# Sixteen column pairs of the last FFN's first product by Strassen, with weight sums made partly by DMA

## Chip, cores and metric

The kernel runs on one core of a Trainium2 chip. The metric is device time in microseconds, the median of the runs shown. Before the change it is 1356.94 us over three runs, 1356.64 to 1357.12.

## What is computed

A trunk of two layers on a sequence of 512 tokens with a model width of 1024: a gated short convolution, an FFN, an SSD mixer, an FFN, each between RMSNorms and with shift, scale and gate from a conditioning vector. The change lies in the last FFN alone, whose width DFF is 2816:

```python
def swiglu_ffn(h, w_in, w_out):
    gate, up = jnp.split(h @ w_in, 2, axis=-1)
    return (jax.nn.silu(gate) * up) @ w_out
```

All data are float32. The kernel splits each operand of a matmul into a high part rounded to the narrower fp32r and a low part (value minus high part), and adds three matmuls (high x high, high x low, low x high) for each product.

## The kernel before

The features of the first product lie on partitions, the 512 tokens along the free dimension. `w_in` has 22 gate and 22 up chunks of 128 columns. A chunk is `in_chunk` (L289): eight k tiles of 128 rows, each with three matmuls of 128x512 (`mm3`, L276 to L278), 24 in all. Six chunks are begun while the sub-layer before ends (the lead, `li`) and finished by `rest(i)` with 256-wide matmuls; two more (`more`) have weights ready; the last FFN's own loop (L1661 on) does the others, 38 whole chunks together with those two.

For each pair of chunks `load_pair` loads 1 MB of weights with one DMA from the SP queue into a buffer of the pool `wst` (two buffers), in rows of 256 columns. ACT copies a chunk's weights to their high part (L221), DVE subtracts for the low part (L222), into a buffer of the pool `whl` (four buffers). `gate` (L1583) puts the SiLU of a finished chunk on ACT, `up` (L1591) multiplies on DVE into `raw`, and after each fourth chunk `s13` (L1587) makes two differences of halves of `raw` on DVE. These are the first operands of the second product.

The second product, `raw` times `w_out`, is already done in the Strassen-Winograd form: seven products (`PRODUCTS`, L1537) over eleven pairs p of row blocks, 77 steps taken two at a time (`products(n)`, n from 0 to 38), each step six matmuls of 128x512 (L1650). The weights' sums t1, t2, t3 and t4 are made in place in SBUF: t1, t2 and t4 by DMAs from the POOL queue that add what they carry to what lies there (L1657), t3 by loading two blocks of `w_out` a second time, one on the ACT queue (L1664), one added from the POOL queue. `w_prep(n)` and `a_prep(n)` split the operands on ACT and DVE (L1615, L1616, L1628, L1629), four and three tiles ahead. `behind(n)` places the sums and the ends of the output blocks.

`w_out` is 11.5 MB. Before the change units 0, 1 and 2 (pairs 0 to 4; tiles `w2t0` to `w2t2`) are loaded during the loop, units 3 and 4 into `wst` buffers near its end, and units 5 to 10 into the space of the activations `h` when the last chunk has read them (L1710).

In this stage the order of the work is written out by hand: a `manual_schedule` holds for PE, SP, ACT, DVE and POOL, so each engine does its instructions in the order of the source and waits for each in turn. The pools `fo` and `fb` of this stage take the space of the phase that closes with the lead.

Of the kernel before, what the change touches and what calls it, by code (L numbers as in the profile page):

```python
# [8 lines left out]
F32 = mybir.dt.float32  # L9
# [7 lines left out]
P = 128  # L17
# [18 lines left out]
def trunk_kernel(  # L36
# [252 lines left out]
    def in_chunk(w, h):  # L289
        pst = mm_ps("ip")  # L290
        mm_chunk(pst, w, h)
        return pst
# [277 lines left out]
    with ExitStack() as ph:  # L570
# [112 lines left out]
        with tc.manual_schedule(engines={PE_ENGINE, mybir.EngineType.SP, mybir.EngineType.Activation,  # L683
# [858 lines left out]
    with ExitStack() as ph:  # L1542
# [4 lines left out]
        NP = NF // 2  # L1547
        ws, splits, gates = list(more), [(), ()], {}
# [11 lines left out]
        def w2_load(i):  # L1560

            u = units[i]
            t = w2t[i] if i < 3 else wst_p.tile([P, 1, 2, D], F32, tag="wst", name="w2s")
            for q in range(len(u)):
                dma(t[:, q, :, :], w2_rows(u[q])[:, 0])
            rows_of[i] = (t[:, :, 0, :], t[:, :, 1, :])

# [11 lines left out]

        def load_pair(p):  # L1580
            ws.extend(load_w([(w1, p % 2 * DFF + (4 + p // 2 * 2) * P, 256)], later=splits))

        def gate(f, pst):  # L1583
# [6 lines left out]

        def up(f, pst):  # L1591
            dve.tensor_mul(raw[:, f, :], pst, gates[f])
            if f % 4 == 3:
                s13(f // 2 - 1, 2)
            elif f == NF - 1:
                s13(f // 2, 1)


# [54 lines left out]
        with tc.manual_schedule(engines={PE_ENGINE, mybir.EngineType.SP, mybir.EngineType.Activation,  # L1653
                                         mybir.EngineType.DVE, mybir.EngineType.Pool}):

            def add_(dst, src):
                pool.dma_start(dst, src, accum_op=ADD)  # L1657

            def t1(i):
                add_(b_(i, "b12"), b_(i, "b11"))  # L1660

            def t3_load(i):
                for q, p in enumerate(units[i]):
                    dma_s(b_(i, "b11", q), w2_rows(p)[:, 0, 0, T:])  # L1664

            def t3(i):
                for q, p in enumerate(units[i]):
                    add_(b_(i, "b11", q), w2_rows(p)[:, 0, 1, T:])

# [5 lines left out]

            load_pair(0)
# [3 lines left out]
            tiles = []  # L1680
            K = 2 * NF - 6
            for k in range(K):
                if k % 2 == 0 and k < K - 4:
                    load_pair(k // 2 + 1)
                if k in (8, 14, 20):
                    w2_load((8, 14, 20).index(k))
                if k in (K - 4, K - 2):
                    w2_load(3 + (k - K + 4) // 2)
                if k in (K - 12, K - 10, K - 8):
                    t1((k - K + 12) // 2)  # L1690
                tiles.append(in_chunk(ws[k], h))
                q, j = divmod(k - 3, 4)
                if j < 2 and k > 2:
                    gate(4 + 2 * q + j, tiles[k - 1])
                elif k:
                    up(2 + 2 * q + j, tiles[k - 1])
                if k < K - 2:
                    for op in splits[k + 2]:
                        op()
                else:  # L1700
                    a_prep(k - K + 2)
                    w_prep(k - K + 2)
            up(NF - 1, tiles[-1])
# [4 lines left out]
            for c, r in ((0, 0), (0, 1), (1, 0), (1, 1)):  # L1708
                for i in range(5, len(units)):
                    dma(rows_of[i][r][:, 0, c * T:(c + 1) * T], w2_rows(units[i][0])[:, 0, r, c * T:(c + 1) * T])  # L1710
            for n in (2, 3):
                w_prep(n)
            a_prep(2)
            for i in range(3, len(units)):
                t1(i)
# [27 lines left out]
            def behind(n):  # L1743

                for i, u in enumerate(units):
                    if n - 8 == u[-1] // 2:
                        t2_(i)
                    if n == 8 + i:
                        t3_load(i)
                    if n == 17:  # L1750
                        t3(i)
                if n == 18:
                    for i in range(len(units)):
                        t4(i)
                for t in range(2):
# [85 lines left out]
```

## Time and profile before

| what | before |
|---|---|
| median of 3 runs | 1356.94 us |
| profiled execution: span | 1355.3 us |
| granted TensorE clock, mean | 0.997 |
| lead's last matmuls / first products' loop | until 1032.1 / 1032.1 to 1238.6 us |
| second product and end | 1238.6 to 1355.3 us |

The span runs from the first to the last instruction of one profiled execution; the median of the runs lies 1.6 us above it, which is the time around the span. PE is TensorE's matmul, PEld its weight load, DVE the vector engine, ACT the scalar engine, POOL GpSimd; SP issues most DMAs. In a group's row stand the line, the engine, the operation, the tile written and those read, the shapes, the count, then busy time and mean ns, then the engine's idle time before and what ended it. Windows give the busy time (and count) of each engine in a stretch of the span. Times in a timeline are start and duration in microseconds.

### The profile page before, as it was taken

Reading aid. Unit: us, or ns where it says so; the run is one execution under the profiler, and the core shown is the slowest. Engines: PE = TensorE matmul, PEld = TensorE weight load, DVE = VectorE, ACT = ScalarE, POOL = GpSimd, SP = SyncE. Lnnn points to the kernel's source line nnn. Section 1 sums busy time; section 2 is a strip of 40 time slices with the busy share of each in tenths; the row PEclk is TensorE's granted clock in tenths of the full one; section 3 lists DMA queues with packets and bytes.
Section 4 is the critical chain, followed back from the end, with each engine's and each line's share of the span. In section 5 each row is a group of like instructions: output and inputs, shape, how many; then the busy total and the mean of one; then the engine's idle time right before and its main releaser. Section 6 shows DMA issues by size and latency. Waiting matters only on the chain.

```text
span 1355.3 us, 17419 instructions
## 1 busy us (share of the span) xinstructions
PE 1339.1 (99%) x6909; PEld 1126.9 (83%) x6909; DVE 898.7 (66%) x1437; ACT 570.1 (42%) x893; POOL 47.0 (3%) x61
## 2 busy tenths in 40 slices
PE   8999999999999999999999999999999999999996
PEld 6788889888888888898888888888899888888885
DVE  5588866777777322658988998897673233336877
ACT  5333355232222211655554455564472212224664
POOL 0000000000000000000000000000000000001231
PEclk9999999999999999999999999999999999999998
DMA  9757760777786323415434334323311455326685
GB/s 311 233 180 231 247 202 4 242 237 245 227 257 201 110 94 94 128 33 162 137 122 128 107 96 132 117 78 121 129 62 63 156 171 172 98 96 196 159 148 120
DMA packets 160565, 204.77 MB, mean 151 GB/s; under 512 B 6868, under 2 KB 112228, under 8 KB 159460
## 3 DMA queue, kind: packets, MB, share of 16 engines
q1 hardware_dynamic: 148512, 176.34, 41.2%
q0 software_dynamic: 6240, 11.54, 5.1%
q10 hardware_dynamic: 5732, 15.79, 3.6%
q8 instruction: 54, 0.88, 0.3%
q14 instruction: 27, 0.22, 0.1%
HBM read 192.75 MB, written 2.24 MB: 144 GB/s over the span
## 4 chain that ended last, share of the span: by engine, by line
PE 93%; issue 2%; SPq 2%; DMA 1%; DVE 1%; ACT 1%; POOL 0%; DVEq 0%; POOLq 0%; ACTq 0%
PE ip L276 19%; PE ip L278 18%; PE ip L277 18%; PE y L378 6%; PE y L379 6%; PE y L380 6%; PE cA L1650 3%; PE li L276 3%; PE li L278 3%; PE li L277 3%; PE li L756 1%; PE yd L1283 1%; PE cD L1650 1%; SPq L611 1%; PE yo L1277 1%
## 5 line engine op out<-in xcount | busy, mean ns | idle before, releaser
L276 PE MATMUL ip<-h,whl 128*128 128x512 f32 x1096 | 431.1, 393 | 0.2 <-DVE cv L863 0.2
L278 PE MATMUL ip<-h,whl 128*128 128x512 f32 x1096 | 427.2, 390 | 0.0
L277 PE MATMUL ip<-h,whl 128*128 128x512 f32 x1096 | 426.8, 389 | 0.0
L222 DVE TENSOR_TENSOR whl<-wst,whl 128x1024 fp32r<-128x1024 f32 x132 | 160.7, 1221 | 133.4 <-ACT whl L221 133.2
L276 PEld LDWEIGHTS ip<-h,whl 128*128 128x128 f32 x1096 | 205.9, 188 | 43.9 <-issue 1.8
L278 PEld LDWEIGHTS ip<-h,whl 128*128 128x128 f32 x1096 | 205.8, 188 | 43.2
L277 PEld LDWEIGHTS ip<-h,whl 128*128 128x128 f32 x1096 | 206.0, 188 | 41.8
L221 ACT CAST whl<-wst 128x1024 fp32r<-128x1024 f32 x132 | 136.6, 1042 | 32.5 <-PE ip L278 23.7
L124 DVE SCALAR_TENSOR_TENSOR ada_acc<-ada_st,csil,ada_acc 128x512 f32<-128x512 f32 x140 | 105.0, 750 | 3.5
L204 DVE TENSOR_TENSOR whlo<-wsto,whlo 128x1024 fp32r<-128x1024 f32 x41 | 49.9, 1224 | 78.5 <-ACT whlo L203 78.4
L276 PE MATMUL li<-h,whl 128*128 128x256 f32 x288 | 83.3, 289 | 0.0
L278 PE MATMUL li<-h,whl 128*128 128x256 f32 x288 | 81.7, 284 | 0.0
L277 PE MATMUL li<-h,whl 128*128 128x256 f32 x288 | 81.6, 283 | 0.0
L203 ACT CAST whlo<-wsto 128x1024 fp32r<-128x1024 f32 x41 | 42.6, 1049 | 76.5 <-PE y L380 71.3
L378 PE MATMUL y<-whlo,ff 128*128 128x512 f32 x176 | 68.7, 390 | 0.0
L380 PE MATMUL y<-whlo,ff 128*128 128x512 f32 x176 | 68.5, 389 | 0.0
L379 PE MATMUL y<-whlo,ff 128*128 128x512 f32 x176 | 68.5, 389 | 0.0
L1142 DVE SCALAR_TENSOR_TENSOR cu<-ip,cols,cu 128x511 f32<-128x511 f32 (+2 forms) x84 | 62.8, 748 | 3.9 <-ACT cu L1139 1.4
L1585 ACT ACTIVATE g<-ip 128x512 f32<-128x512 f32 x18 | 10.8, 598 | 122.1 <-PE ip L278 122.1
L1650 PE MATMUL cA<-whlo,ao 128*128 128x512 f32 x264 | 61.1, 390 | 0.8 <-ACT whlo L1615 0.8
L1650 PEld LDWEIGHTS cA<-whlo,ao 128*128 128x128 f32 x264 | 49.5, 188 | 11.4 <-ACT whlo L1615 1.2
L276 PEld LDWEIGHTS li<-h,whl 128*128 128x128 f32 x288 | 55.3, 192 | 0.0
(281 smaller groups left out, 1928.2 us busy)
## 6 DMA issues: line engine op xcount, KB each, us to landing
ada_st<-in_ada_w_dram SPq DMA_DIRECT2D x96, 512.0 KB, 5.0
wst<-in_f_w_in_dram SPq DMA_DIRECT2D x44, 1024.0 KB, 5.9
wst<-in_m_w_in_dram SPq DMA_DIRECT2D x14, 1024.0 KB, 5.3
wsto<-in_f_w_out_dram SPq DMA_DIRECT2D x10, 1024.0 KB, 5.0
wst<-in_m_w_in_dram SPq DMA_DIRECT2D x20, 512.0 KB, 5.1
wst<-in_a_w_in_dram SPq DMA_DIRECT2D x9, 1024.0 KB, 6.0
csb<-cs_d ACTq DMA_DIRECT2D x8, 1024.0 KB, 5.5
wsto<-in_m_w_out_dram SPq DMA_DIRECT2D x7, 1024.0 KB, 6.5
```

The costliest lines, as they stand in the source:

```text
L124: dve.scalar_tensor_tensor(acc, w, csil[:, k:k + 1], acc, MUL, ADD)
L204: dve.tensor_tensor(dst[:, 1, :nk, :], src, dst[:, 0, :nk, :].bitcast(F32), SUB)
L221: later.append((lambda sw=sw, w=w: act.copy(w[:, 0, :nk, :], sw), lambda sw=sw, w=w: dve.tensor_tensor(w[:, 1, :nk, :], sw, w[:, 0, :nk, : ...
L222: lambda sw=sw, w=w: dve.tensor_tensor(w[:, 1, :nk, :], sw, w[:, 0, :nk, :].bitcast(F32), SUB)))
L276: pe.matmul(dst, w_at(w, 0, kk), a[:, 0, sl], start=start, stop=False)
L277: pe.matmul(dst, w_at(w, 0, kk), a[:, 1, sl], start=False, stop=False)
L278: pe.matmul(dst, w_at(w, 1, kk), a[:, 0, sl], start=False, stop=stop)
L378: pe.matmul(pst, a[:, 0, tk], wt[:, 0, kk, :], start=k == 0, stop=False)
L379: pe.matmul(pst, a[:, 0, tk], wt[:, 1, kk, :], start=False, stop=False)
L380: pe.matmul(pst, a[:, 1, tk], wt[:, 0, kk, :], start=False, stop=k == K - 1)
L1142: dve.scalar_tensor_tensor(u[:, sft:], pst[:, :T - sft], w[3 - sft], u[:, sft:], MUL, ADD)
L1650: pe.matmul(bank[r][sub], a[:, al, q, tk], w[:, hl, q, :], start=first and k == 0, stop=last and k == 2, skip_group_check=True)
```

## The change

Sixteen column pairs (units u = 0 to 15, even u gate columns, odd u up columns) of the first product are computed by seven products of 12 matmuls of 128x256 each, over halves of k, of the pair's columns and of the tokens. Four chunks and the two of `more` stay as they were.

For the moving operands the activations are added up again from their two parts (`value`), combined to four new operands T and split (`t_one` to `t_four`); two raw quadrants of `h` serve as the others. For the weights X is the first chunk, Y, S and Z are sums. `fetch(u)` issues up to five DMAs from SP in rows of 128 columns, and two adding DMAs from POOL; two more sums are made on DVE (`sum_y`, `sum_s`). Z's chunk is loaded a second time, one unit later. The accumulators are gathered by ACT and DVE (`keep`, `c11`, `c12`, `c22`, `c21`).

The T operands and the sums take the space of `w2t0` to `w2t2`, so all of `w_out` is loaded from the end of unit 15 on, by quadrants in the order of their use. t3 becomes a subtraction on POOL (b22 after t2, minus b11), and its second loads go.

```diff
-        w2t = [fb.tile([P, 2, 2, D], F32, tag=f"w2t{i}", name=f"w2t{i}") for i in range(2)]
-        w2t += [fb.tile([P, 1, 2, D], F32, tag="w2t2", name="w2t2")]
+        tq = [fb.tile([P, 2, 2, 4, 256], F32R, tag=f"w2t{i}", name=f"tq{i}") for i in range(2)]
+        sums_w = fb.tile([P, 2, 2, 4, P], F32, tag="w2t2", name="sg")
...
+        def fetch(u):
+
+            st, sg = wst_p.tile([P, 16, P], F32, tag="wst", name="wsu"), sums_w[:, u % 2]
+            staged[u] = st, sg
+            if u < UN:
+                dma(sg[:, 0], w1_cols(u, 1, 0))
+                dma(sg[:, 1], w1_cols(u, 1, 1))
+            if u:
+                dma(st[:, 8:12, :], w1_cols(u - 1, 1, 0))
+            dma(st[:, 0:8, :], w1_cols(u, 0))
+            if u:
+                dma(st[:, 12:16, :], w1_cols(u - 1, 1, 1))
+            if u < UN:
+                add_(flat2(sg[:, 0]), flat2(sg[:, 1]))
+            if u:
+                add_(flat2(st[:, 8:12, :]), flat2(staged[u - 1][0][:, 0:4, :]))
...
+        def split(dst, src):
+            act.copy(dst[:, 0], src)
+            dve.tensor_tensor(dst[:, 1], src, dst[:, 0].bitcast(F32), SUB)
...
+        def sum_y(u):
+            st, sg = staged[u]
+            dve.tensor_add(sg[:, 1], sg[:, 0], st[:, 0:4, :])
...
+            dst, w = banks[r, u][:, LO], wts[kind, u]
+            for k in range(4):
+                for i, (wl, al) in enumerate(((0, 0), (0, 1), (1, 0))):
+                    pe.matmul(dst, w[:, wl, k0 + k, :], moving(q, k, al), skip_group_check=True,
...
-            def t3(i):
-                for q, p in enumerate(units[i]):
-                    add_(b_(i, "b11", q), w2_rows(p)[:, 0, 1, T:])
+            def t3(p):
+                i = unit_of[p]
+                q = units[i].index(p)
+                pool.tensor_tensor(b_(i, "b11", q), b_(i, "b22", q), b_(i, "b11", q), SUB)
...
             for i, f in ((0, 0), (2, 0), (1, 1), (3, 1), (4, 2), (5, 3)):
                 rest(i)
-                (up if i in (2, 3) else gate)(f, lead_ps[i])
...
+                if i in (2, 3):
+                    up(f, lead_ps[i])
+                else:
+                    gate(f, lead_ps[i])
+                if i == 1:
+                    for j in range(4):
+                        value(j)
+                elif i == 3:
+                    t_one()
+                elif i == 4:
+                    for j in range(4, 8):
+                        value(j)
+            acc = in_chunk(more[0], h)
+            split_x(0)
+            for b in range(2):
+                t_two(b)
+            sum_y(0)
+            split_y(0)
+            t_three()
+            fetch(1)
+            acc2 = in_chunk(more[1], h)
+            sum_s(0)
+            up(2, acc)
+            split_s(0)
+            for u in range(UN):
...
+                    fetch(u + 2)
...
+                product(u, "P1")
+                if u:
+                    c12(v)
+                else:
+                    up(3, acc2)
+                    for b in range(2):
+                        t_four(b)
+                split_x(u + 1)
+                if u:
+                    product(v, "P7")
+                keep(u, "A", 0, LO)
+                product(u, "P5")
+                if u:
+                    c22(v)
+                product(u, "P2")
+                keep(u, "C", 1, HI)
+                if u:
+                    product(v, "P4")
+                c11(u)
+                split_z(u)
+                if not last:
+                    sum_y(u + 1)
+                    sum_s(u + 1)
+                product(u, "P6")
+                if u:
+                    c21(v)
...
+                    split_y(u + 1)
+                product(u, "P3")
+                keep(u, "A", 0, HI)
+                if not last:
+                    split_s(u + 1)
```

More of the change, by code (lines that the diff above doesn't have):

```diff
@@ new lines, in out_of, with keep, c11, c12 @@
+        def out_of(u, f):
+            if (u, f) not in outs:
+                outs[u, f] = raw[:, 4 + u // 2 * 2 + f, :] if u % 2 else t2("g")
+            return outs[u, f]
+        def keep(u, r, f, part):
+            act.copy(out_of(u, f)[:, part], banks[r, u][:, LO])
+        def c11(u):
+            dve.tensor_add(out_of(u, 0)[:, LO], banks["B", u][:, LO], out_of(u, 0)[:, LO])
+        def c12(u):
+            o, f = out_of(u, 0), 4 + u // 2 * 2
+            dve.tensor_add(o[:, HI], banks["C", u][:, LO], o[:, HI])
+            if u % 2:
+                dve.tensor_mul(o, o, gates[f])
+            else:
+                gates[f] = o
+                act.activation(o, o, AF.Silu)
@@ L1682, in trunk_kernel @@
[L1682 to L1698, printed above, removed]
+                if i in (2, 3):
+                    up(f, lead_ps[i])
+                else:
+                    gate(f, lead_ps[i])
@@ L1713, in trunk_kernel @@
             a_prep(2)
-            for i in range(3, len(units)):
+            for i in (0, 2, 1, *range(3, len(units))):
                 t1(i)
```

186 lines of the change are left out of this document (155 added, 31 removed).

## The prediction

> **What bounds the kernel now.** I read the page first, then the stretches of the last FFN.
>
> ```profile
> span 1355.3 us, 17419 instructions
> PE 1339.1 (99%) x6909; PEld 1126.9 (83%) x6909; DVE 898.7 (66%) x1437; ACT 570.1 (42%) x893; POOL 47.0 (3%) x61
> ...
> q1 hardware_dynamic: 148512, 176.34, 41.2%
> q0 software_dynamic: 6240, 11.54, 5.1%
> ...
> PE 93%; issue 2%; SPq 2%; DMA 1%; DVE 1%; ACT 1%; POOL 0%; DVEq 0%; POOLq 0%; ACTq 0%
> ...
> L222 DVE TENSOR_TENSOR whl<-wst,whl 128x1024 fp32r<-128x1024 f32 x132 | 160.7, 1221 | 133.4 <-ACT whl L221 133.2
> ```
>
> PE is busy throughout and is 93% of the chain. A microsecond of PE work removed is a microsecond gained, unless another engine or a DMA then ends last. The median of the runs, 1356.94, is 1.6 above this span; I add that 1.6 again at the end.
>
> The busy times of the stretches (columns PE, PEld, DVE, ACT, POOL, granted clock, DMA share, GB/s), first column pairs, then the second product:
>
> ```profile
> 1032.10:1237.90 205.80, 205.80 (x909) 170.45 (x909) 68.76 (x73) 50.31 (x61) 5.20 (x5) 1.00 0.41 129
> 1238.60:1345.20 106.60, 105.43 (x463) 86.35 (x462) 84.67 (x135) 68.56 (x123) 30.23 (x33) 1.00 0.75 159
> ```
>
> In the first, 38 chunks of the first product, PE never waits, DVE works a third of the time and the DMAs 41%. One 128x512 matmul advances every 205.80/909 = 0.2264 us. That is the room the change spends.
>
> **The gain in matmuls.** A column pair is now two chunks, 48 matmuls of width 512: 48 x 0.2264 = 10.87 us. Afterwards it is seven products of 4 k x 3 = 12 matmuls of width 256. The rate of that width, with the same order of weights and operands, stands in the lead before this stage:
>
> ```profile
> 1020.15 0.28 PE L277 MATMUL li<-h,whl 128*128 128x256 f32 x1
> ...
> 1021.59 0.28 PE L277 MATMUL li<-h,whl 128*128 128x256 f32 x1
> ```
>
> These starts are 12 matmuls apart: 1.44 us, one product. Half the width costs 0.120, not 0.113. Seven products take 10.08 us, so a pair saves 0.79 and sixteen save **12.6 us**. An eighth fewer multiplications gives only 7%, since the width's fixed part is paid twice.
>
> **The setup.** The sums of activations (eight sums hi+lo, four operands T, each split again) and the first weights are made on DVE and ACT in program order, behind the first `up`. When can DVE start?
>
> ```profile
> 1017.26 2.36 DVE L204 TENSOR_TENSOR whl<-wst,whl 128x1024 fp32r<-128x1024 f32 x2 [0.52 <-ACT whl L203]
> 1032.19 1.29 DVE L1592 TENSOR_TENSOR raw<-li,g 128x512 f32<-128x512 f32 x2 [12.57 <-PE li L278]
> ...
> 1240.39 0.68 DVE L1616 TENSOR_TENSOR whlo<-w2t,whlo 128x512 fp32r<-128x512 f32 x1
> 1240.99 0.68 DVE L1616 TENSOR_TENSOR whlo<-w2s,whlo 128x512 fp32r<-128x512 f32 x1
> ```
>
> ```profile
> 1013.75 0.41 ACT L508 CAST h<-u 128x256 fp32r<-128x256 f32 x1
> 1016.18 1.99 ACT L203 CAST whl<-wst 128x1024 fp32r<-128x1024 f32 x2
> 1021.32 0.60 ACT L1585 ACTIVATE g<-li 128x512 f32<-128x512 f32 x1 [1.84 <-PE li L278]
> ```
>
> DVE idles 12.57 us and starts `raw` only at 1032.19, with the very last lead matmul, though ACT had the first gate at 1021.32 and its partner chunk ends a few microseconds later. `raw` takes over space of the phase that closes with the lead, so its first writer waits for the lead's last matmul. In the change `up(0)` is still the first of these DVE operations, and the sums are queued behind it. So everything starts at 1032.19, while PE has only two whole chunks left (48 x 0.2264 = 10.87, to 1043.0).
>
> The DVE queue from there, at 0.60 a step for width 512 (1240.39 to 1240.99), 1.14 for width 1024 (two in 2.36, the last 1.22), 0.03 for each hand-over and ACT at 0.62 and 1.04 for the same widths (0.95 a step):
>
> - two `up` and four sums: 3.7
> - first T: subtract 1.22, ACT 1.04, low part 1.14: 3.45
> - four sums 2.4, low part of X(0) 1.14
> - second T in two halves, each 0.69 + 0.69 + ACT 0.62 + 0.60 + hand-overs: 5.4
> - sum_y 0.69 and ACT's copy of Y(0) 1.04: 1.8
>
> That is 17.9: P5(0) starts at 1050.1. PE has done P1(0) by 1044.4 and waits 5.7; after two matmuls it waits 1.0 more for Y's low part. P5 and P2 then last to 1054.0. DVE meanwhile does the third T, sum_s, `up(2)`, S(0), `up(3)`, s13 and the two halves of the fourth T, with ACT between: 1.14 + 0.60 + 0.77 + 0.60 + 0.72 + 0.72 + 0.60, then 0.72 + 0.65 + 0.61 + 0.71 + 0.55. Only behind them stand ACT's X(1) (0.97) and keep (0.41), for which P6(0) waits: 1060.9, a wait of 7.0. P7(0) and P4(0) wait 0.55 and 0.75 for Z(0) and c22, since `fetch(1)` could not write its buffer before the third T had read it. The setup costs 5.7 + 1.0 + 7.0 + 0.55 + 0.75 = **15.0 us** of PE. Its cover is two chunks; nearly three more would be needed to hide it.
>
> Such waits have a second price:
>
> ```profile
> 1345.00:1347.00 2.00, 0.55 (x3) 0.13 (x1) 1.96 (x4) 0.98 (x3) 0.00 (x0) 1.00 0.45 170
> 1347.00:1348.00 1.00, 0.00 (x0) 0.00 (x0) 0.96 (x3) 0.00 (x0) 0.00 (x0) 0.90 0.68 258
> 1348.00:1350.00 2.00, 0.00 (x0) 0.00 (x0) 1.96 (x5) 0.00 (x0) 0.00 (x0) 0.50 0.36 133
> ```
>
> The granted clock falls to 0.50 some 2.3 us after PE's last matmul at 1345.5. A wait of 7.0 will lose it as well; P6(0) and P3(0), 2.9 us, then run up to twice as long, but the next waits, 0.55 and 0.75, are DVE's and hide 1.3 of that. I put **0.4**, a quarter of the way from 0 (all hidden) to 1.6 (2.9 doubled, less 1.3). The Trainium skill (TensorE: Matmul & The Clock Gate, "Part 1: The HAM clock gate") says that an idle window of about 3.4 us halves the clock and a busy one of that length gives it back. By that, as an estimate, 1.7 us would be lost before cover, which leaves the 0.4; the rows show the fall, and none shows the return after a wait.
>
> **The steady units.** DVE per unit: three splits of 1024 (3 x 1.14), one of 512 (0.60), two sums (0.69 each), three sums from PSUM of width 256 (0.43 each by this row),
>
> ```profile
> 1239.59 0.43 DVE L1588 TENSOR_TENSOR s1t<-raw 128x256 f32<-128x256 f32 x1
> ```
>
> together 6.7; odd units add two products of 0.60, and every fourth unit the two subtractions s13 of 0.72: 6.7, 7.9, 6.7, 9.3 of 10.08. It fits, but in order. I stepped the queue through a unit: without s13, P4 finds c22 ready 0.28 before it needs it; with s13 the low parts of Y, S and X and then c22 come 1.44 later, and PE waits 1.16. This happens in units 4, 8 and 12: **3.5 us**. Bounds: 0 if the steps are a little shorter, 7 if hand-overs eat the 0.28 in the other units.
>
> The DMAs. A unit loads 1.57 MB in rows of 512 bytes and adds 2 x 256 KB inside SBUF. The same row length in another stage, and the landing times:
>
> ```profile
> 550.00:555.00 5.00, 5.00 (x24) 4.15 (x23) 3.01 (x4) 2.81 (x5) 0.00 (x0) 1.00 1.07 292
> ```
>
> ```profile
> wst<-in_m_w_in_dram SPq DMA_DIRECT2D x20, 512.0 KB, 5.1
> ...
> w2t<-w2t POOLq DMA_DIRECT2D x6, 512.0 KB, 6.1
> ...
> w2s<-w2s POOLq DMA_DIRECT2D x6, 256.0 KB, 3.7
> ```
>
> At 292 GB/s the loads take 5.4 us; an added packet takes 5.1% x 16 x 1355.3 / 6240 = 177 ns, 256 of them over 16 engines 2.8 us: 8.2 of 10.08. From issue, load and add land after about 5.1 + 3.7 = 8.8 to 10; they are wanted some 13 after it. SP issues five and POOL two per unit, nothing else stands in those queues. Cost **0**, with 3 us of slack; above it, a rival.
>
> **The second product.** 104.5 us of matmuls are unchanged. Its weights, 11.5 MB, now all load after unit 15 (SP: 27 issues, in the order of use). Before the first of these products PE has P3(15), P7, P4 and four chunks, 26 us, and about 4.6 MB are wanted by then, 16 us at 292 GB/s. The additions t1 come later and t2 meets them in POOL's queue; before, that place had the second loads for t3, which are gone. There the chain has a wait on t2 already:
>
> ```profile
> 1273.08 5.66 DMA w2t<-w2t
> 1278.76 0.63 ACT whlo L1615
> 1279.41 0.55 DVE whlo L1616
> 1280.02 0.69 DVE ao L1629
> 1280.76 3.24 PE cC L1650 x13
> ```
>
> PE loses about 0.8 there now; I take it as unchanged, **0**, between -1 and +2.5. The new subtractions t3 run on POOL:
>
> ```profile
> L1299 POOL TENSOR_TENSOR accg<-accg,sqg 128x512 f32<-128x512 f32 x7 | 9.1, 1298 | 879.2 <-ACT sqg L1297 879.2
> ```
>
> Eleven x 1.30, one each 2.72 us of PE, beside t4's issue: done long before product 5 reads them.
>
> **Sum.** 1355.3 - 12.6 + 15.0 + 0.4 + 3.5 = 1361.6; with the 1.6 outside the span, **1363.2 us**, 0.46% slower. About 0.2%, 2.7 us, is what a measurement of this kernel can tell from no change.
>
> **Rivals.**
> 1. *The setup is hidden.* If the sums ran in DVE's idle 12.57 us, or PE had other work, 15.4 would go: 1356.9 - 12.6 + 3.5 = 1347.8, faster. For it: DVE is idle there. Against it: the order puts `up(0)` first, and that row waits to 1032.19. It decides when over 10 of the 15 us are covered. Chance 0.08.
> 2. *Half hidden*: shorter steps, or matmul stalls that overlap; some 5 us less: 1358. Chance 0.13.
> 3. *The loop becomes bound by its DMAs*, each add waiting behind loads and loads behind adds. It decides at 10.08 us per unit; if 8.2 grows by a third to 10.8, fourteen units pay 0.7: 1373. For it: share 1.07 of the engines in the row above. Chance 0.13.
> 4. *POOL holds DVE up.* DVE has 1.8 us of work per 2.72 step in the second product; if it stood still for each t3 of 1.30, it would fall 0.4 behind a step, 4 over eleven, less what the preparation three steps ahead absorbs: 1367 at worst. No row has both with two SBUF inputs. The Trainium skill (SBUF — State Buffer, "Who interferes with whom") says that a DVE instruction with two SBUF inputs and a GpSimd one that reads SBUF block each other in full; no run here shows it. Chance 0.06.
>
> **How the numbers follow.** My forecast has 0.60 and of itself 1360 to 1367. Faster than 1354.2: rival 1, 0.08. Within 0.2%: most of rival 2, 0.12. Slower: 0.80. The range 1357 to 1370 leaves out rival 1 and the upper part of rival 3.
>
> **What would show it.** Right: two PE waits of 5 to 8 us between 1043 and 1062 that end on DVE or ACT, DVE busy without a break from 1032, three waits near 1.2 us one every four units, units of 10.1 otherwise, and a second product of about 106.6. Wrong: no long wait after the lead (rival 1); waits on `wsu` or `sg` DMAs in every unit (rival 3); a product that doesn't take 1.44; DVE operations stretched beside t3 (rival 4).

## The result, and the profile after

The changed kernel takes **1380.53 us** (median of four runs, 1380.38 to 1383.27), the kernel before 1356.8 beside it: 1.0179 times as long, 95% interval 1.0165 to 1.0194. The forecast was 1363.2 with a range from 1357 to 1370: the sign was right, the size was not. The profiled execution grew from 1355.3 to 1378.3, by 23.0 us.

The page of the changed kernel: span, busy times, shares of the chain.

```profile
span 1378.3 us, 19120 instructions
PE 1337.6 (97%) x7485; PEld 1151.1 (84%) x7485; DVE 998.5 (72%) x1570; ACT 618.6 (45%) x995; POOL 80.0 (6%) x93
...
PE 82%; DVE 6%; DMA 4%; issue 3%; SPq 2%; ACT 2%; POOL 1%; DVEq 0%; POOLq 0%; ACTq 0%
```

PE is busy 1.5 us less than before, in a span 23.0 longer; its share of the chain fell from 93% to 82%. Where did it wait? The first rows of the view of waits, PE alone: engine, tile and line, what ended the wait, us in total, times, longest.

```profile
PE cD L1778 <- DVE ao L1757: 9.3, 2, 5.9
PE sC L1687 <- ACT whl L1642: 5.7, 1, 5.7
PE sA L1687 <- ACT g L1697: 4.6, 1, 4.6
PE sA L1687 <- DVE g L1713: 3.1, 3, 1.0
```

The three rows of `s` tiles are the first product, and they are the waits that the prediction named. The row above them, in the second product (`cD`), is the one that it priced at nothing. By stages, columns as before:

```profile
1032.10:1246.60 214.50, 200.75 (x1490) 193.65 (x1489) 150.16 (x206) 99.40 (x164) 28.06 (x32) 0.96 0.73 186
1246.60:1368.00 121.40, 109.94 (x463) 88.44 (x461) 103.55 (x135) 68.47 (x123) 38.50 (x36) 0.96 0.54 123
```

The first product ends at 1246.6 instead of 1238.7, 7.9 later, where 6.3 were forecast. The second product, with the same 77 steps of six matmuls, takes 121.4 us from its first matmul to its last instead of 106.9: **14.5** of the 23.0. (The last 0.5 lie behind its last matmul.) Its matmuls became slower too: PE is busy 109.94 us in it, before 105.43, since the granted clock fell to 0.50 with each of the two long waits. DVE shows 103.55 us of work in it, before 84.67, with the same 135 instructions: they became longer. The timeline of DVE where PE waits:

```profile
1305.39 2.80 DVE L1744 TENSOR_TENSOR whlo<-w2t,whlo 128x1024 fp32r<-128x1024 f32 x1
1308.12 4.48 DVE L1757 TENSOR_TENSOR ao<-s1t,ao 128x512 fp32r<-128x512 f32 x1
1312.53 7.26 DVE L1744 TENSOR_TENSOR whlo<-w2t,whlo 128x512 fp32r<-128x512 f32 x1
1319.71 1.74 DVE L1744 TENSOR_TENSOR whlo<-w2s,whlo 128x512 fp32r<-128x512 f32 x1
```

and of POOL at the same time:

```profile
1310.17 1.87 POOL L1790 TENSOR_TENSOR w2s<-w2s 128x512 f32<-128x512 f32 x1
1311.38 1.50 POOL L1619 DMA_DIRECT2D w2h<-w2h  x1
1311.99 2.21 POOL L1790 TENSOR_TENSOR w2s<-w2s 128x512 f32<-128x512 f32 x1
1313.69 1.34 POOL L1619 DMA_DIRECT2D w2h<-w2h  x1
1314.30 2.04 POOL L1790 TENSOR_TENSOR w2h<-w2h,w2h 128x512 f32<-128x512 f32 x1
...
1317.98 4.57 POOL L1790 TENSOR_TENSOR w2h<-w2h,w2h 128x512 f32<-128x512 f32 x2
```

Operations of 0.68 us last 4.48 and 7.26 while POOL runs t3 (L1790) and issues t4 (L1619) without a break. The profile counts the time in which DVE stands still as busy time; the length of an operation, or the mean of a group, against the same form elsewhere gives it away.

The profile's spans of POOL operations are rough, so below the starts of POOL's operations count for more than their lengths.

### The profile page after: what moved, and what is told of

The parts are those of the page before. It is cut to its first block, busy times and chain, and to the rows that moved or that the text cites. A ratio compares the mean times of both kernels' runs of the same rounds, so it can differ in the third digit from the quotient of the medians.

```text
span 1378.3 us, 19120 instructions
## 1 busy us (share of the span) xinstructions
PE 1337.6 (97%) x7485; PEld 1151.1 (84%) x7485; DVE 998.5 (72%) x1570; ACT 618.6 (45%) x995; POOL 80.0 (6%) x93
## 4 chain that ended last, share of the span: by engine, by line
PE 82%; DVE 6%; DMA 4%; issue 3%; SPq 2%; ACT 2%; POOL 1%; DVEq 0%; POOLq 0%; ACTq 0%
PE ip L276 14%; PE ip L278 14%; PE ip L277 14%; PE y L378 6%; PE y L379 6%; PE y L380 6%; PE sA L1687 4%; PE li L276 3%; PE li L278 3%; PE li L277 3%; DMA wsu<-in_f_w_in_dram 2%; PE sC L1687 2%; PE li L756 1%; DVE whlo L1744 1%; PE yd L1283 1%
## 5 line engine op out<-in xcount | busy, mean ns | idle before, releaser
L276 PE MATMUL ip<-h,whl 128*128 128x512 f32 x840 | 331.3, 394 | 0.2 <-DVE cv L863 0.2
L278 PE MATMUL ip<-h,whl 128*128 128x512 f32 x840 | 327.2, 390 | 0.0
L277 PE MATMUL ip<-h,whl 128*128 128x512 f32 x840 | 327.0, 389 | 0.0
L276 PEld LDWEIGHTS ip<-h,whl 128*128 128x128 f32 x840 | 157.8, 188 | 33.7 <-issue 1.8
L278 PEld LDWEIGHTS ip<-h,whl 128*128 128x128 f32 x840 | 157.7, 188 | 33.3
L277 PEld LDWEIGHTS ip<-h,whl 128*128 128x128 f32 x840 | 157.8, 188 | 31.7
L222 DVE TENSOR_TENSOR whl<-wst,whl 128x1024 fp32r<-128x1024 f32 x99 | 120.4, 1221 | 60.1 <-ACT whl L221 60.0
L221 ACT CAST whl<-wst 128x1024 fp32r<-128x1024 f32 x99 | 103.0, 1041 | 4.5 <-DMA wst<-in_m_w_in_dram 2.6
L1687 PE MATMUL sA<-tq,whl 128*128 128x256 f32 x576 | 76.1, 287 | 7.6 <-ACT g L1697 4.6
L1687 PEld LDWEIGHTS sA<-tq,whl 128*128 128x128 f32 x576 | 72.7, 195 | 8.7 <-ACT g L1697 4.9
L1299 POOL TENSOR_TENSOR accg<-accg,sqg 128x512 f32<-128x512 f32 x7 | 9.1, 1297 | 879.3 <-ACT sqg L1297 879.3
```

The costliest lines, as they stand in the source:

```text
L221: later.append((lambda sw=sw, w=w: act.copy(w[:, 0, :nk, :], sw), lambda sw=sw, w=w: dve.tensor_tensor(w[:, 1, :nk, :], sw, w[:, 0, :nk, : ...
L222: lambda sw=sw, w=w: dve.tensor_tensor(w[:, 1, :nk, :], sw, w[:, 0, :nk, :].bitcast(F32), SUB)))
L276: pe.matmul(dst, w_at(w, 0, kk), a[:, 0, sl], start=start, stop=False)
L277: pe.matmul(dst, w_at(w, 0, kk), a[:, 1, sl], start=False, stop=False)
L278: pe.matmul(dst, w_at(w, 1, kk), a[:, 0, sl], start=False, stop=stop)
L1687: pe.matmul(dst, w[:, wl, k0 + k, :], moving(q, k, al), skip_group_check=True, start=q in ("P1", "P5", "P2") and k == 0 and i == 0, stop=k ...
```

## Experiments: the second product

Each run in these sections is one execution, unless a number of runs is given; the effects read from them are several microseconds, while the four runs of the change lie within 2.9.

Two theories. L (lock): t3 on POOL and DVE's operations hold each other up. W (late weights): w_out is loaded, and its sums are made, too late; the long DVE operations only show it.

**t3 on DVE instead of POOL.**

```diff
-                pool.tensor_tensor(b_(i, "b11", q), b_(i, "b22", q), b_(i, "b11", q), SUB)
+                dve.tensor_tensor(b_(i, "b11", q), b_(i, "b22", q), b_(i, "b11", q), SUB)
```

> The change with one edit: the eleven subtractions t3 run on DVE, at the same place in the program, instead of POOL. Theory L (lock): POOL's tensor_tensor and DVE's hold each other up; that made the second product 121.4 us instead of 106.9. By L it falls to 107 to 110 (DVE gets 11 x 0.6 = 6.6 us more work, and it has room), the span from 1378.3 to 1364 to 1367, and no DVE operation of width 512 is over 0.8 us. Rival W (late weights): w_out is loaded and added up too late, the long DVE operations only show it; then the second product stays at 118 us or more and the span above 1375.

1366.46 us; span 1364.6, 13.7 less than in the change. The second product, and t3 itself (the view by line of code):

```profile
1246.46:1354.60 108.14, 105.72 (x463) 86.30 (x461) 90.88 (x146) 68.52 (x123) 23.61 (x25) 1.00 0.61 138
```

```profile
L1790 DVE TENSOR_TENSOR w2t<-w2t x5: 684/694/696, 1291.7 to 1301.3; 128x512 f32<-128x512 f32 x5
```

DVE does eleven instructions more in 12.7 us less, each t3 in 0.69, and no operation of width 512 is long. L holds. 1.3 us stay against before: a wait of 1.6 in product C, where the kernel before has one of 0.3.

**t3 by second loads, as before.** The functions `t3_load` and `t3`, and the places of t3 and t4, are those of the kernel before; nothing else.

> The change, but t3 as in the kernel before: two blocks of w_out loaded a second time, one added by DMA; POOL makes no tensor_tensor. All else is the change. L: second product 107 to 110, span 1364 to 1368, although the DMAs move 5.8 MB more. W: 5.8 MB more make late weights later, second product 120 to 125, span 1377 to 1382.

1372.88 us, span 1371.1, the second product 114.8. Between the two: no DVE operation is long, but PE waits 5.6 us in product C for an operand queued behind weights that wait for t2. So the later loading is not free either as soon as 5.8 MB more go through the same stretch. W is right for this variant, and for about 1 us of the change, where that wait is 1.1.

**t3 on POOL in the kernel before.** The reverse of the last edit, in the kernel before.

> The kernel before, with one part of the change alone: t3 as eleven subtractions on POOL, t4 placed as in the change; the weights are loaded as early as before, the first product is untouched. L: DVE operations beside t3 last 1.5 to 4 us, and the second product takes 109 to 120 instead of 106.9: span 1358 to 1369. W: weights are in time, so nothing is lost: span 1354.5 to 1356.5.

1369.63 us; span 1367.8, 12.5 more than before, the second product 119.5. One DVE operation lasts 7.79, more than the 4 that were expected. This part of the change alone costs 12.5 us, most of what the forecast missed. The first three t3 of this run stand 3.9 and 5.8 us apart, and beside each of them a DVE operation of 0.68 lasts 2.16 to 3.12: even a spaced t3 held DVE up for 1.5 to 2.4, not 1.30.

## Experiments: why DVE stood still so long

If a t3 delays a DVE operation by its own length, that gives some 2.5 us, not 7.3. So trains of the same subtraction were put where DVE works a third of the time, in the first product's loop of the kernel before; they write tiles that nobody reads.

```diff
+                    if k in (10, 14, 18, 22):
+                        for m in range({10: 1, 14: 2, 18: 4, 22: 8}[k]):
+                            pool.tensor_tensor(junk, raw[:, 2 + 2 * q + j, :], h[m][:, 0, :].bitcast(F32), SUB)
```

> The kernel before, with fifteen more POOL subtractions of 128x512 (two SBUF inputs, into a tile nobody reads) in the first product's loop, where DVE works a third of the time: trains of 1, 2, 4 and 8 behind up of chunks 7, 9, 11 and 13. Theory L1 (POOL keeps the way to SBUF as long as its next instruction is ready): a DVE operation that meets a train stands still to its end, so the longest DVE operation grows with the train: about 2.5, 4, 6 to 7 and 10 to 13 us. Rival L2 (they take turns): no DVE operation is over 3.5 us, whatever the train, and only their number grows. The span changes by under 6 us in both.

1356.83 us, span 1355.1. No DVE operation was over 2.4 us, even beside the train of eight: they took turns, instruction by instruction. L1 fell for trains of this kind, in which every subtraction writes the same tile and so waits for the one ahead. Was it the DMA issue between them? The next run has eight pairs of subtraction and issue, and ahead of them (not printed) four subtractions alone, each into a place of its own:

```diff
+                    if k == 22:
+                        for m in range(8):
+                            pool.tensor_tensor(junk[0][:, 0].rearrange("p c t -> p (c t)"), raw[:, 13, :], h[m][:, 0, :].bitcast(F32), SUB)
+                            add_(junk[1 + m // 4][:, m % 4 // 2, m % 2], h[m][:, 0, LO].bitcast(F32))
```

> The kernel before, with two trains on POOL in the first product's loop, into tiles that nobody reads: behind chunk 7 four subtractions of 128x512 alone, behind chunk 13 eight subtractions, each followed by the issue of a DMA that adds 128x256 inside SBUF, as t3 and t4 alternate in the change. The trains without DMAs showed DVE and POOL taking turns: no DVE operation over 2.4 us. Theory L3 (in a train of subtraction and issue POOL leaves no gap, since it issues the next DMA while the subtraction runs): in the second train a DVE operation of 1.22 stands still to near the train's end, 5 to 15 us, in the first at most 2.5. Rival L4 (turns are kept there too; t3 hurts because DVE itself works without a pause in the second product): at most 3.5 us in both trains.

1356.87 us. In both trains the longest DVE operation was 2.3 to 2.6 us. L3 fell too, in this form: each subtraction of the second train still waited for the one ahead, which wrote the same tile. The four of the first train did not wait for one another and had no issue ahead; beside them the longest was 2.31.

**t4 behind all t3**, in the change:

```diff
                 if 14 <= n < 14 + NP:
                     t3(n - 14)
-                    if n - 14 < len(units):
-                        t4(n - 14)
+                if n == 25:
+                    for i in range(len(units)):
+                        t4(i)
```

> The change with one edit: the additions t4 are issued together at step 25, behind all t3, instead of one behind each t3. t3 stays on POOL. L3 (the pair of subtraction and issue shuts DVE out): DVE and POOL take turns, DVE operations beside t3 last at most 3 us, the second product takes 108 to 113 us instead of 121.4, span 1365 to 1370. L4 (eleven t3 close together beside a busy DVE are enough): second product 117 us or more, span 1374 or more.

1381.63 us, the second product 122.7: without issues between the t3 it is no better, as L4 had it. DVE, then POOL:

```profile
1294.85 14.97 DVE L1744 TENSOR_TENSOR whlo<-w2s,whlo 128x512 fp32r<-128x512 f32 x2 [0.92 <-ACT whlo L1743]
1309.74 0.68 DVE L1757 TENSOR_TENSOR ao<-raw,ao 128x512 fp32r<-128x512 f32 x1
```

```profile
1294.26 0.86 POOL L1619 DMA_DIRECT2D w2h<-w2h  x1 [1.10 <-DVE ao L1757]
1294.82 6.56 POOL L1790 TENSOR_TENSOR w2t<-w2t 128x512 f32<-128x512 f32 x5
1301.06 2.75 POOL L1790 TENSOR_TENSOR w2s<-w2s 128x512 f32<-128x512 f32 x2
1303.50 5.16 POOL L1790 TENSOR_TENSOR w2h<-w2h,w2h 128x512 f32<-128x512 f32 x4
1308.36 1.47 POOL L1619 DMA_DIRECT2D w2t<-w2t  x1
```

Two splits of 0.68 take 14.97 us: the first of them lasts 14.37, the whole train of eleven (14.97 less a step of 0.60). PE waits 10.2. What differs from the trains in the loop is seen in the starts: the eleven t3 start 1.22 to 1.26 apart, while each record lasts 1.5 to 1.6, so each starts 0.3 to 0.35 before the one ahead ends. In the train of eight in the loop each started 0.08 after it. In the change itself the issues stand between: the t3 of 1308.34 ends at 1309.90 and the next starts at 1310.17, but each issue starts before the t3 ahead ends and each t3 before that issue ends, so POOL has no pause there either. This led to theory L6, that DVE gets in only where POOL pauses, and to three trains of five:

```diff
+                    if k in (10, 18, 26):
+                        seen = raw[:, 2 + 2 * q + j, :]
+                        if k != 18:
+                            add_(junk[0][:, 0, int(k == 26)], seen[:, LO])
+                        for m in range(1, 6):
+                            n = 1 if k == 26 else m
+                            to = junk[n // 2][:, n % 2].rearrange("p c t -> p (c t)") if k > 10 else raw[:, 16 + m, :]
+                            pool.tensor_tensor(to, seen, h[0][:, 0, :].bitcast(F32), SUB)
```

> The kernel before, with three trains of five POOL subtractions of 128x512 in the first product's loop, into rows and tiles that nobody reads, behind chunks 7, 11 and 15. A: a DMA issue just ahead, the five independent of each other. B: independent, no issue ahead. C: an issue ahead, and each writes where its predecessor wrote, so that it waits for its end. In the trace so far, subtractions that start 0.35 us before the one ahead ends shut DVE out, and those that start at or after its end don't. Theory L6 (a subtraction that needn't wait overlaps its predecessor, and DVE gets in only in a gap): a DVE operation of 0.6 or 1.2 us stands still to the train's end, over 4 us, in A and perhaps in B; in C none is over 2.6. Rival L7 (it is DVE's unbroken work in the second product): none over 2.6 us in any of the three.

1356.61 us. Train A (an issue ahead, independent), B (independent), C (an issue ahead, each waits for the one ahead); DVE:

```profile
1087.75 7.30 DVE L1589 TENSOR_TENSOR raw<-raw 128x512 f32<-128x512 f32 x1
...
1132.85 2.31 DVE L222 TENSOR_TENSOR whl<-wst,whl 128x1024 fp32r<-128x1024 f32 x1
...
1174.79 2.39 DVE L1589 TENSOR_TENSOR raw<-raw 128x512 f32<-128x512 f32 x1
1177.10 2.31 DVE L222 TENSOR_TENSOR whl<-wst,whl 128x1024 fp32r<-128x1024 f32 x1
```

and the trains:

```profile
1087.30 0.89 POOL L1657 DMA_DIRECT2D junk<-raw  x1 [20.17 <-DVE raw L1592]
1087.89 6.60 POOL L1709 TENSOR_TENSOR raw<-raw,h 128x512 f32<-128x512 f32 x5
...
1130.59 9.21 POOL L1709 TENSOR_TENSOR junk<-raw,h 128x512 f32<-128x512 f32 x5 [36.10 <-DVE raw L1592]
...
1174.99 9.16 POOL L1709 TENSOR_TENSOR junk<-raw,h 128x512 f32<-128x512 f32 x5
```

In A, DVE stands still to the end of the train, and the five take 6.60 us. In B and C DVE gets in between, at most 2.31 and 2.39 us an operation, and the five take 9.2. So by these trains both are needed: members that needn't wait for each other, and an issue that runs into the first one (1087.30 to 1088.19, over the start at 1087.89). The first is also shown by the run with gaps that follows. The second rests on A alone against B and the four of the run of pairs, and A differs in one more thing: it writes rows of `raw`, they write tiles of another pool. L7 fell: the loop gives the same stall as the second product.

The cross-check in the change, with t4 behind all t3 and a gap behind each t3:

```diff
+                pool.tensor_tensor(tiny, b_(i, "b11", q)[:, 0:2], b_(i, "b11", q)[:, 0:2], SUB)
```

> The change with t4 behind all t3 (the run in which a DVE operation stood still for 14.4 us) and one thing more: behind each t3 a POOL subtraction of two columns that reads what the t3 wrote, so it waits for its end; its output is read by nobody. POOL does more, not less. L6: a gap opens behind each t3, DVE takes its turns, no DVE operation is over 3 us, the second product takes 108 to 113 us instead of 121 to 123: span 1365 to 1370. L7: nothing changes or it gets worse, span 1379 or more.

1371.53 us, span 1369.4: POOL does 22 subtractions instead of eleven, and 10.1 us are won against the run without the gaps. DVE and POOL:

```profile
1297.45 1.78 DVE L1757 TENSOR_TENSOR ao<-raw,ao 128x512 fp32r<-128x512 f32 x1
...
1301.46 0.68 DVE L1757 TENSOR_TENSOR ao<-raw,ao 128x512 fp32r<-128x512 f32 x1
```

```profile
1294.73 1.63 POOL L1790 TENSOR_TENSOR w2t<-w2t 128x512 f32<-128x512 f32 x1
1296.44 0.53 POOL L1791 TENSOR_TENSOR ss<-w2t 128x2 f32<-128x2 f32 x1
1296.94 1.74 POOL L1790 TENSOR_TENSOR w2t<-w2t 128x512 f32<-128x512 f32 x1
```

Between 1296.36 and 1296.44 there is a gap, and DVE has its turn in each: 1.78 for one that meets a t3, 0.68 for the next. The longest DVE operation lasts 2.11. The second product takes 113.6, just over what L6 gave; PE's wait in product C is 2.5 in this run.

## Experiments: the first product

**The pairs s13 of units 3, 7 and 11 made one unit later, while PE is in an odd unit.**

```diff
                 dve.tensor_mul(o, o, gates[f])
-                raw_done(f)
+                if u == UN - 1:
+                    raw_done(f)
             else:
+                if u:
+                    raw_done(f - 2)
```

> The change with one edit: the pairs of subtractions s13 of units 3, 7, 11 are made one unit later, in the odd unit, where DVE has 6.7 us of work instead of 7.9. By the prediction the three waits of 1.18 us in units 4, 8 and 12 vanish and none comes instead: the first product ends 3.5 us sooner, span 1374.3 to 1375.3. If those waits came from the weights' sums by DMA they stay: span 1377.5 to 1379.

1376.6 us, span 1374.5. The three waits of 1.0 are gone and nothing came instead in the first product: from P1(0) to the second product 199.6 us instead of 203.6.

**The setup in another order.** Operations as in the change; what is made first for P5(0) comes first, `up(0)` and `up(1)` later, and the sums lie in unused rows of `raw`:

```diff
-            va = wst_p.tile([P, 4, T], F32, tag="wst", name="va")
-            vb = [fo.tile([P, 2, T], F32, tag="ao", name="vb") for _ in range(2)]
+            va = raw[:, 18:22, :]
+            vb = [raw[:, 14 + 2 * b:16 + 2 * b, :] for b in range(2)]
             fetch(0)
+            fetch(1)
```

```diff
-                if i in (2, 3):
-                    up(f, lead_ps[i])
-                else:
+                if i not in (2, 3):
                     gate(f, lead_ps[i])
...
+            for j in range(4):
+                value(j)
+            dve.tensor_tensor(va[:, :, LO], va[:, :, LO], va[:, :, HI], SUB)
             split_x(0)
...
+            t_low(tq_of(0, slice(0, 4)), va[:, :, LO])
             sum_y(0)
...
+            up(0, lead_ps[2])
+            up(1, lead_ps[3])
...
+            product(0, "P1")
+            keep(0, "A", 0, LO)
+            product(0, "P2")
+            product(0, "P5")
+            for j in range(4, 8):
+                value(j)
```

> The change with the order of its setup alone altered: first T, X(0) and Y(0) are made first, the two first products up(0) and up(1) and the other sums later, P2(0) before P5(0), the first banks' copies ahead of the fourth T, and the added-up activations lie in unused rows of raw, so that unit 1 loads at once. The same operations in another order, t3 on POOL as in the change. Theory Q: the setup's 16.6 us (six products that take 25.3 instead of 8.6) come from the order of DVE's and ACT's queues; then P7(0) starts 11 to 14 us sooner and the span is 1364 to 1367.5. Rival D: the amount of DVE work after 1032, or the loads and adds of unit 1, sets it; then under 6 us are won, span above 1372.

1379.44 us. P7(0) starts at 1052.1 instead of 1068.3, sixteen us sooner, but new waits of 2.6 and 4.8 us in unit 1 leave the first product only 4.0 sooner, and the second takes 2.9 longer (124.2; its longest DVE operations are 7.79, 5.15 and 4.51). The span is one that rival D had foretold. (In this run unit 2's loads overwrote sums of unit 0 that were still to be read; in the next and in the first of the runs together the SiLU of half a chunk came before P2's part was added. Operations, sizes and counts are the same; the times are those of these orders, and what the right order alone would have changed in them wasn't measured.)

Then unit 1 was put in order by hand as well:

> As the run before, with unit 1 put in order too: up(3), the subtractions and high parts of the fourth T, c22(0) ahead of the other sums, P2(1) before P5(1), s13(0, 2) last. t3 stays on POOL as in the change. Theory Q (the setup's 16.6 us come from the order of the queues): P7(0) starts at 1052 as in the run before and the later waits of that run, 2.6 and 4.8 us, shrink to under 2 together; the first product ends 13 to 15.5 us sooner than in the change, span 1362.5 to 1366. Rival D (DVE simply has more work than PE after 1032): waits move on and the first product ends at most 8 us sooner, span 1370 or more.

1375.13 us: the first product 8.3 sooner, the second 3.0 longer, close to what D had foretold; a wait of 2.9 appears in unit 2, where a copy on ACT stood behind one that waits for DVE.

And the start of unit 2, by the place of a few lines:

```diff
+            split_z(1)
+            product(1, "P6")
+            c21(0)
+            keep(1, "A", 0, HI)
+            sum_y(2)
...
             c12(0)
-            c11(0)
             c11(1)
-            split_z(1)
-            sum_y(2)
```

> As the second setup run, with the wait of 2.9 us in unit 2 taken away: the copy of bank A(1) ahead of Y(2) on ACT, Z(1) and sum_y(2) ahead of c11 and c12 on DVE, s13(0, 2) two units later. t3 stays on POOL. Theory Q: that wait and the slow matmuls behind it cost 5.8 us, nothing new appears, the first product ends 13 to 14.5 us sooner than in the change (1232 to 1233.5). Rival D (DVE has more to do than PE in the first three units, so a wait moves on): first product ends at 1236 or later.

1369.37 us, span 1367.5. The second product starts at 1234.45, 12.1 sooner, between what Q and D had foretold; a wait of 1.6 is left in unit 2. The order of the queues, theory Q, accounts for some 12 of the 16.6 us. Each time the wait moved on and became smaller; whether the rest is the amount of DVE's work (D) or an order not yet found is open.

**Together.** First the three edits (t3 on DVE, this setup's second form, s13):

> The change with the three edits together: t3 on DVE, setup and unit 1 in the new order, s13 one unit later. If the three losses (13.7, 14 to 15, 3.5 us) are separate and add up: 1380.5 less 31 to 32 is 1348 to 1350 us, 0.5 to 0.65% faster than the kernel before. If one covers another (DVE gets 6.6 us more in the second product, or weights land later against a first product that ends 18 us sooner): 1352 to 1358.

1354.88 us over ten runs, 0.9984 times the kernel before, interval 0.9974 to 0.9994: what the three gains measured above add up to (13.7, 8.3 and 4.0), and less than was hoped of the setup. Then with the third form of the setup, and at step 12 the activations ahead of the weights that wait for t2:

> All together: the new setup, s13 one unit later, t3 on DVE, and at step 12 the activations' tile prepared ahead of the weights' tile that waits for t2. If what the single edits gave adds up: 1380.5 - 13.7 (t3) - 14 (setup) - 3.8 (s13) - 1.3 (the wait for t2) = 1347 to 1349 us, faster than the kernel before by 0.6 to 0.7%; if the setup's wait only moves on, 1351 to 1354.

1351.41 us, 0.9959 (0.9946 to 0.9973). The swap at step 12 won nothing: product C waits 1.9 and 0.6 us, on two steps, where it waited 1.3 without the swap.

```diff
-            for i in (0, 2, 1, *range(3, len(units))):
+            for i in (0, 2, 1, 3, 4):
                 t1(i)
...
+                if 10 <= n <= 11:
+                    t1(2 * n - 15)
+                    t1(2 * n - 14)
```

> The best kernel so far (setup, s13, t3 on DVE; without the swap at step 12, which only moved its wait) with two more edits: in unit 2, c22(1) and P4's operand ahead of X(3) and S(2) on DVE, so the wait of 1.6 us there goes; and the additions t1 of the last four units behind t2 of the first three on POOL's queue. If the waits of 1.6 and 2.4 us in the run before come from these orders: span 1345 to 1346.5, time 1347 to 1348.5. If t2 is late because the weights land late, the second stays: 1349 to 1350.5.

1350.7 us, 0.9946 (0.9932 to 0.996), more than was expected. With t1 of the last four of the nine units of `w_out` (5 to 8; pairs 7 to 10) behind the first t2, product C has no wait left and the second product takes 106.3. But with the new order of unit 2 (not printed), which also issues `fetch(4)` later, there were five waits of 0.2 to 0.6 in units 3 to 5, and the first product ended 2.0 later.

Last, t1's new place, with unit 2 as it was in the run of 1351.41 us:

> The best kernel with t1 of the last four units behind t2 of the first three on POOL's queue, and unit 2 as it was two runs before (its wait of 1.6 us is back). If the small waits of units 3 to 5 in the last run came from fetch(4) issued later, they go, the first product ends near 1230.5, and the second takes 106.3: span 1346.5 to 1347.5, time 1348 to 1349.5. If they came with t1's place, they stay: span 1349 or more.

**1349.05 us** (1348.98 to 1350.26), 0.9945 times the kernel before, interval 0.9932 to 0.9959. That is 7.9 of the 12.6 us that the matmuls save. From P1(0) to the second product it takes 187.8 us, where sixteen pairs of 10.08 and four chunks of 5.43 make 183.0; the other 4.8 are waits and slow matmuls in the first three units. With unit 2 as it was the waits of units 3 to 5 are gone; the second product takes 107.0, 0.7 more than was expected. The page and the second product:

```profile
span 1347.2 us, 19129 instructions
PE 1328.5 (99%) x7485; PEld 1143.8 (85%) x7485; DVE 984.7 (73%) x1581; ACT 618.7 (46%) x995; POOL 65.2 (5%) x82
```

```profile
1230.20:1337.20 107.00, 106.07 (x463) 86.14 (x461) 91.00 (x146) 68.57 (x123) 23.62 (x25) 1.00 0.61 139
```

## Why the prediction was wrong

**The step that failed: the second product at 0, and in it "Eleven x 1.30, one each 2.72 us of PE ... done long before product 5 reads them".** With t3 on POOL the second product took 121.4 us, with t3 on DVE 108.2; of the span it was 13.7. Two things in the step were wrong.

The eleven t3 came late. POOL's queue still held t1 and t2, the first t3 ran at 1294.1, and the last nine ran between 1303 and 1323 with t4's issues among them, so POOL had hardly a pause.

And rival 4, which named the mechanism, was priced as if DVE got in after every t3, "0.4 behind a step, 4 over eleven". That is about the rate with gaps: in the run with the small subtraction DVE operations grew by 1.1, the first by 1.4, and the second product took 5.4 more than with t3 on DVE. Without a pause of POOL, DVE gets nothing for several t3: two of them in the operation of 4.48, four in the one of 7.26, and all five and all eleven in the operations of 7.30 and 14.37 of the trains without issues between. The Trainium skill (SBUF — State Buffer, "Who interferes with whom") says that such a pair of instructions blocks in full; the trace agrees for one pair (0.68 becomes 1.78). The chance of 0.06 was too low for a mechanism that could cost this much where DVE has little time to spare. The time to spare was also put too high, with 1.8 us of work per step of 2.72: the kernel before has 19.69 us of DVE in the 26.80 from 1284.9 on, 2.0 a step.

The other steps:

- *Matmuls*: right. Seven products of 1.44, pairs of 10.08, from the timeline of any steady unit.
- *Setup, 15.4 with its clock*: measured 16.6 (P1(0) to P7(0) in 25.28 us, six products of 1.44 are 8.64). By the timeline of PE:

```profile
1043.02 1.60 PE L1687 MATMUL sA<-h,whl 128*128 128x256 f32 x12
1050.28 0.80 PE L1687 MATMUL sC<-tq,whl 128*128 128x256 f32 x2 [5.66 <-ACT whl L1642]
1051.54 2.50 PE L1687 MATMUL sC<-tq,whl 128*128 128x256 f32 x10 [0.46 <-DVE whl L1643]
1053.84 2.76 PE L1687 MATMUL sB<-h,whl 128*128 128x256 f32 x12
1061.16 2.93 PE L1687 MATMUL sA<-tq,whl 128*128 128x256 f32 x12 [4.56 <-ACT g L1697]
1063.89 2.76 PE L1687 MATMUL sC<-h,wss 128*128 128x256 f32 x12
1066.45 2.01 PE L1687 MATMUL sA<-h,whl 128*128 128x256 f32 x12
1068.30 1.60 PE L1687 MATMUL sA<-tq,whl 128*128 128x256 f32 x12
```

  P5(0) was forecast for 1050.1 and came at 1050.28, P6(0) for 1060.9 and came at 1061.16: the queue, stepped through by hand, was right to 0.3 us. The second wait is 4.56, not 7.0, because P5 and P2 ran at half speed ahead of it, and the waits of 0.55 and 0.75 at P7 and P4 were covered by slow matmuls in the same way. What was too small is the clock: from P6(0) to P7(0) 7.14 us pass for 4.32 of work, 2.8 lost, where 0.4 and the two waits came to 1.7.
- *s13, 3.5*: right. Three gaps of 1.18 by the starts of the matmuls, in units 4, 8 and 12; gone in the run that moved s13.
- *DMAs of the loop, 0*: right. No matmul of the first product waits for a load or an added sum; rival 3 did not come. ACT waits twice for a load between 1070 and 1225, 2.2 us in all, and PE does not feel it.
- *Second loads gone, weights later, between -1 and +2.5*: the size was right (1.3 with t3 on DVE), and the reason was the one named, t2 behind t1 in POOL's queue: with t1 of four units behind t2 the wait goes. The 0.8 that PE was said to lose there before is 0.3 in the view of waits.
- *Rivals 1 and 2*: right to give them little. The order decided, as said, and another order hides 12 us of it.

So 6.3 of 7.9 us in the first product were forecast, and none of the 14.5 in the second.

## What to carry to other kernels

Work given to POOL is not free because POOL is idle: where DVE reads two tiles in SBUF, POOL operations that read SBUF hold it up, and a run of independent ones without a pause, with DMA issues ahead of it or in it, shut DVE out for several of them, here up to eleven. Price it as the whole run against DVE's slack, not as one operation. A queue that is late can close up operations that were meant to be spaced; that this made it worse here was not tested by itself. Put such work on DVE where it has room, or open gaps in the run; and read the mean per form of the other engine, since standing still is shown as busy. Where a queue in program order sets a wait, removing it shows the next one: step through the queue until the engine has caught up, here three units.

## What the runs showed of the hardware

- *A run of subtractions as one block.* Above: 14.37 us of standstill for one DVE operation of 0.68, behind eleven POOL subtractions; with a wait between the members, or without an issue ahead, turns. Why an issue sets this off is not shown; that each member of these trains then starts 0.3 to 0.36 us before its predecessor's record ends is. With issues between the subtractions, as in the change, DVE got in after two and after four; what let it in there is not shown.
- *The clock comes back late after some waits.* Short windows of the change (before the comma start, end and length, the granted clock third from the end):

```profile
1046.80:1047.20 0.40, 0.00 (x0) 0.00 (x0) 0.35 (x1) 0.01 (x1) 0.00 (x0) 0.65 0.00 0
...
1056.50:1057.00 0.50, 0.10 (x1) 0.00 (x0) 0.50 (x2) 0.00 (x0) 0.50 (x1) 0.50 1.10 292
...
1057.40:1057.80 0.40, 0.00 (x0) 0.00 (x0) 0.00 (x0) 0.40 (x1) 0.00 (x0) 1.00 1.18 315
...
1067.00:1067.40 0.40, 0.40 (x4) 0.40 (x3) 0.40 (x2) 0.00 (x0) 0.40 (x1) 0.50 1.21 288
1067.40:1067.80 0.40, 0.40 (x5) 0.40 (x5) 0.28 (x1) 0.09 (x1) 0.31 (x1) 1.00 1.21 293
```

  It falls 2.3 us after PE stops (1044.6). PE works again from 1050.3, and full speed returns between 1057.0 and 1057.4, in the next wait, where it is no use; the second time PE works from 1061.1 and it returns at 1067.4. Over 6 us from the start of work to full speed each time; after the wait of 4.56 that cost 2.8 us. In the second product it is shorter: PE works from 1312.66 and the clock is back at 1316.6, and from 1323.17 and it is back at 1326.8, after 3.9 and 3.6 us. All eight changes of the granted clock from 1046.9 to 1326.8 lie whole multiples of 3.41 us apart (for instance 1057.16, 1060.57 and 1067.40), so it counts where between two such marks the work begins. The Trainium skill (TensorE: Matmul & The Clock Gate, "Part 1: The HAM clock gate") gives about 3.4 us of sustained work and a window of that length that runs free; the marks agree with it, and the two long returns show that from the start of work it can take up to twice that.
- *A POOL operation has a price of its own.* The subtraction of two columns takes 0.53 us, that of 512 columns 1.63 (both in the run with the gaps).
